# A hybrid layer's first unit: statistics, scaling and rounding of x at separate places, the norm in two parts, first loads in a fixed order

## The chip, the cores and the metric

One Trainium2 chip, one core of it. The metric is the device time of one execution, in microseconds (us). Before the change it is 2423.84 us, the median of three runs (2422.58 to 2424.6).

## What is computed

One decoder layer on x (2048 x 1024, float32): a pre-norm, one combined input projection, a gated DeltaNet branch, a sliding-window attention branch in three groups of four heads, gates and an output projection. The change touches the start: the norm of x and the projections of the attention branch.

```python
h = rms_norm(x, norm_w[layer])
proj = h @ w_in[layer]
...
sq = partial_rope(rms_norm(grp(swa_q), q_norm_w[layer][:, None, :]), cos, sin)
sk = partial_rope(rms_norm(grp(swa_k), k_norm_w[layer][:, None, :]), cos, sin)
sv = grp(swa_v)
```

## The kernel before, in words

TensorE works in a reduced float32 format, so each operand is split into a high part (rounded by ScalarE) and a low part (the rest, by a subtraction on VectorE or GpSimd), and each product is three matmuls: high by high, high by low weight, low by high weight (lines 234 to 236 in `s_proj`).

The attention branch comes first, in 12 **units**, one for each group and head. A unit has 16 **tiles** of 128 tokens. A tile is 24 matmuls of 384 columns (8 k-blocks by 3), issued in four **slots** of two k-blocks each. Behind a tile `s_norm` squares the queries and keys (ScalarE, line 245), copies the values, forms the inverse roots on GpSimd (lines 249 and 251, tile `st`), scales queries and keys out of PSUM on VectorE (line 253, `rec`), rotates 32 columns on GpSimd (lines 261 to 264) and writes the record to DRAM (line 265, `rscr`). `rec` and `st` have two buffers, the PSUM tile `mm` has three. The attention of a finished group reads the records back (`a_load`, lines 273 and 274) and works between the slots of later tiles.

The normalised x does not exist when the kernel starts. The **first unit** makes it, tile by tile, in 16 x events. An event c consists of: the sum of squares of the rows (ScalarE, line 109, `xst`) and its inverse root on GpSimd (lines 110 and 112); a diagonal matrix of these roots (ScalarE, line 116, `dg`); a matmul that spreads them over all partitions (line 120, `tp`); eight scalings of the transposed x (VectorE, line 126, `xc`); the high part (ScalarE, line 131, `hh`, two instructions); the low part (line 135, `hl`: five k-blocks on VectorE, three on GpSimd). Event 0 is written out in `swa`, mixed with the eight blocks of the first unit's weights (`high`, line 186, and `low`, line 189: even blocks on VectorE, odd ones on GpSimd). Events 1 to 15 are called in `swa` between the slots, event c behind the first slot whose number reaches 3.5 (c - 1); `x_event(c)` then issues all at once: the diagonal of event c + 1, the statistics of event c + 2, the load of x for event c + 4, and the matmul, scaling, high and low parts of its own.

The weights of the next unit come through three buffers (`raw`); for unit 2 they are split behind tiles 13 to 15 of the first unit (`w384`, lines 78 and 79).

The order on TensorE, ScalarE, VectorE and GpSimd is the order in which the code issues (`manual_schedule`), and each engine runs its queue in order. The order of the DMAs on SyncE's queue is chosen by the framework's scheduler in the version before.

Of the kernel before, what the change touches and what calls it, by code (L numbers as in the profile page):

```python
# [8 lines left out]
AF = mybir.ActivationFunctionType  # L9
# [6 lines left out]
KT = D // P  # L16
NB = 4
H = 4
# [18 lines left out]
def dr(ap, off, dims):  # L37
    return bass.AP(tensor=ap.tensor, offset=ap.offset + off, ap=[list(d) for d in dims])


class Net:
# [94 lines left out]
                          in1=self.hhf[:, n, k0:k1, c:c + P], op=ALU.subtract)  # L136

    def x_event(self, c):
        if c + 1 < 16:
            self.x_diag(c + 1)  # L140
        if c + 2 < 16:
            self.x_stat(c + 2)
            self.x_nat(c + 4)
        rows = self.x_rows(c)
        self.x_scale(c, rows, 0, KT)
        self.x_high(c, 0, 4)
        self.x_high(c, 4, KT)
# [90 lines left out]
    def s_norm(self, s):  # L238
        nc, sp, g, t = self.nc, self.sp, s["g"], s["t"]
        pr = s["pr"]  # L240
        st = sp.tile([P, 4], F32, name="st", bufs=2)
        rec = sp.tile([P, 3, P], F32, name="rec", bufs=2)
        qk, v = rec[:, 0:2, :], rec[:, 2, :]
        for j in range(2):
            nc.scalar.activation(qk[:, j, :], pr[:, j * P:(j + 1) * P], AF.Square, accum_out=st[:, j:j + 1])  # L245
        nc.scalar.activation(v, pr[:, 256:384], AF.Copy)
        if (s["h"], g) == AB_UNIT:
            nc.vector.tensor_copy(self.ab[:, :, t], pr[:, 384:392])
        nc.gpsimd.tensor_scalar(out=st[:, 0:2], in0=st[:, 0:2], scalar1=1.0 / P, scalar2=EPS,  # L249
                                op0=ALU.mult, op1=ALU.add)  # L250
        nc.gpsimd.tensor_tensor(out=st[:, 2:4], in0=st[:, 0:2], in1=self.mhalf[:, 0:2], op=ALU.pow)  # L251
        for j in range(2):
            nc.vector.scalar_tensor_tensor(out=qk[:, j, :], in0=pr[:, j * P:(j + 1) * P], scalar=st[:, 2 + j:3 + j],  # L253
                                           in1=s["w"][2][:, j, :], op0=ALU.mult, op1=ALU.mult)
# [6 lines left out]
        nc.gpsimd.tensor_tensor(out=t1, in0=x, in1=cb, op=ALU.mult)  # L261
# [3 lines left out]
        nc.sync.dma_start(dr(self.rscr[s["h"]][g], t * P * 384, [[384, P], [1, 384]]), rec.rearrange("p a c -> p (a c)"))  # L265
# [77 lines left out]
    def att_slots(self, step, which):  # L343
        for a in self.att:
            d = step - a["at"]
            if "qk" not in a and (d == 0 or (d == -2 and which == 0)):
                self.a_load(a)
            if which == 0 and d == 2:
                self.a_ptrans(a)
            elif which == 1 and d == 1:  # L350
                self.a_score(a)
            elif which == 2 and d == 2:
                self.a_pv(a)
            elif which == 2 and d == 0:
                self.a_trans(a)
        self.att = [a for a in self.att if step - a["at"] < 4]

    def swa(self, units, wps, xctx):
        nc = self.nc
        step = self.step  # L360
        nu = len(units)
        w0, load, high, low = self.w_first(wps[0](), *units[0])
        w = {0: w0}
        for _ in range(2):
            load()
        self.x_nat(1)
        self.warm(26)
        self.x_stat(0)
        self.x_diag(0)
        rows = self.x_rows(0)  # L370
        load()
        self.x_chan(1)
        load()
        high(0)
        low(0)
        for k in (0, 2):
            self.x_scale(0, rows, k, k + 2)
            self.x_high(0, k, k + 2)
        high(1)
        low(1)  # L380
        self.x_low(0, 0, 4, nc.vector)
        for k in (4, 6):
            self.x_scale(0, rows, k, k + 2)
            self.x_high(0, k, k + 2)
        self.x_low(0, 4, 8, nc.gpsimd)
        self.xc.pop(0)
        self.x_nat(2)
# [16 lines left out]
        nc.sync.dma_start(self.rope, self.i["rope"])  # L404
        nc.sync.dma_start(self.mask, self.i["mask"])
        xq = list(range(1, 16))
        for u in range(nu):
            gen = None
            for t in range(16):
                s = dict(h=units[u][0], g=units[u][1], t=t, pr=None, w=w[u])  # L410
                for j in range(4):
                    self.s_proj(s, (2 * j, 2 * j + 1))
                    if j < 3:
                        self.att_slots(step, j)
                    if u == 0 and xq and 4 * t + j >= 3.5 * (xq[0] - 1):
                        self.x_event(xq.pop(0))
                        if not xq:
                            xctx.close()
# [8 lines left out]
                step += 1  # L427
        self.step = step

    def att_drain(self):  # L430
# [566 lines left out]
    def run(self):  # L997
        from functools import partial
        tc = self.tc
        tile_ = dict(reuse_waits="tile")  # L1000
        pool = lambda st, name, side="left": st.enter_context(tc.tile_pool(name=name, bufs=1, side=side, **tile_))
        self.setup()
        sws, wst, xst, late = ExitStack(), ExitStack(), ExitStack(), ExitStack()
        sp = pool(sws, "sp", "right")
        wpa = pool(wst, "wpa")
        self.x_setup(pool(xst, "xp"))
        self.swa_setup(sp)
# [7 lines left out]
        with tc.manual_schedule(engines={E.PE, E.Activation, E.DVE, E.Pool}):  # L1015
            self.swa([(h, g) for g in (2, 1, 0) for h in range(H)], [lambda: (wpa, 392), lambda: (get_b(), 384)], xst)
# [122 lines left out]
```

## Time and profile before

| | us |
|---|---|
| median of three runs | 2423.84 |
| the profiled execution, its own time | 2421.24 |
| span of its instructions | 2419.4 |
| TensorE busy, whole span | 2354.2 (97%) |
| VectorE, ScalarE, GpSimd busy | 1171.0, 854.3, 847.4 |

The profile is one execution. A line of a timeline is: start, duration, engine (PE is TensorE, DVE VectorE, ACT ScalarE, POOL GpSimd, SPq the DMA queue of SyncE), line of the code, operation, tiles (out<-in), count, and in brackets how long the engine had been idle before it and who released it. In the chain of waits a line is start, duration, what; "issue" is time in which nothing that the profile shows was waited for. A line of a stretch is: from and to, length, then the busy time of each engine with its instruction count in brackets, the granted TensorE clock (1 is full), the DMA engines' mean busy share, and GB/s. A busy engine is not an engine at its peak: the ends of pipelined matmuls are modelled.

### The profile page before, as it was taken

What the parts mean: (1) busy time and instruction counts of PE and PEld (TensorE: products, weight loads), DVE (VectorE), ACT (ScalarE), POOL (GpSimd) and SP (SyncE); (2) the same over time, 40 slices, a digit from 0 to 9 for tenths busy, and PEclk for the clock granted to TensorE, in tenths of its full rate; (3) what the DMA queues carried; (4) which work ended last, traced back from release to release, by engine and by line L of the source; (5) the groups of instructions that cost most, each with busy time, mean ns of one, the idle gap of its engine ahead of it and who ended that gap; (6) DMA issues with size and microseconds to landing.
All of it is one profiled execution on the core that took longest, in us unless ns stands there. A gap on an engine that the chain in (4) does not pass through costs nothing.

```text
span 2419.4 us, 40764 instructions
## 1 busy us (share of the span) xinstructions
PE 2354.2 (97%) x13640; PEld 2138.1 (88%) x13640; DVE 1171.0 (48%) x2835; ACT 854.3 (35%) x3005; POOL 847.4 (35%) x1803
## 2 busy tenths in 40 slices
PE   7799999999999999999999999999999999999999
PEld 6699999999999999988777878888888878889998
DVE  4533343334334333343766665999434442454431
ACT  5433333344444434333665663111133313111110
POOL 5634444434333334310433541111123212432441
PEclk8999999999999999999999999999999999999999
DMA  7443444343334334333544443222566555555542
GB/s 257 135 117 106 118 115 118 98 116 109 98 108 113 100 98 120 92 92 98 128 120 110 114 124 113 75 79 66 185 192 194 179 175 154 165 179 153 153 140 75
DMA packets 378810, 307.31 MB, mean 127 GB/s; under 512 B 61352, under 2 KB 345320, under 8 KB 378216
## 3 DMA queue, kind: packets, MB, share of 16 engines
q1 hardware_dynamic: 378312, 304.64, 43.5%
q8 instruction: 108, 1.77, 0.3%
q14 instruction: 102, 0.84, 0.1%
q10 hardware_dynamic: 288, 0.07, 0.0%
HBM read 187.92 MB, written 116.69 MB: 126 GB/s over the span
## 4 chain that ended last, share of the span: by engine, by line
PE 82%; DMA 6%; DVE 5%; POOL 3%; ACT 2%; issue 2%; SPq 0%; ACTq 0%; DVEq 0%; POOLq 0%
PE mm L234 10%; PE mm L236 10%; PE mm L235 10%; PE mm L489 9%; PE mm L491 8%; PE mm L490 8%; DMA gcb<-gcscr 2%; PE mm L962 2%; PE mm L964 2%; PE mm L963 2%; PE mm L981 2%; PE mm L979 2%; PE mm L980 2%; PE po L323 2%; PE tp L280 2%
## 5 line engine op out<-in xcount | busy, mean ns | idle before, releaser
L234 PE MATMUL mm<-wh,hh 128*128 128x384 f32 (+1 forms) x1536 | 557.2, 363 | 9.7 <-DVE rec L253 5.5
L236 PE MATMUL mm<-wh,hl 128*128 128x384 f32 (+1 forms) x1536 | 521.8, 340 | 7.4 <-DVE hl L135 7.4
L235 PE MATMUL mm<-wl,hh 128*128 128x384 f32 (+1 forms) x1536 | 520.1, 339 | 2.4 <-DVE wl L79 2.4
L489 PE MATMUL mm<-hh,wh 128*128 128x512 f32 x1152 | 464.1, 403 | 0.0
L491 PE MATMUL mm<-hh,wl 128*128 128x512 f32 x1152 | 453.7, 394 | 0.0
L490 PE MATMUL mm<-hl,wh 128*128 128x512 f32 x1152 | 452.3, 393 | 0.0
L253 DVE SCALAR_TENSOR_TENSOR rec<-mm,st,wqk 128x128 f32<-128x128 f32 x384 | 117.2, 347 | 393.5 <-POOL st L251 378.7
L234 PEld LDWEIGHTS mm<-wh,hh 128*128 128x128 f32 x1536 | 291.2, 190 | 16.0 <-issue 4.3
L236 PEld LDWEIGHTS mm<-wh,hl 128*128 128x128 f32 x1536 | 290.6, 189 | 9.7 <-DVE hl L135 9.6
L235 PEld LDWEIGHTS mm<-wl,hh 128*128 128x128 f32 x1536 | 292.3, 190 | 3.2 <-DVE wl L79 2.9
L491 PEld LDWEIGHTS mm<-hh,wl 128*128 128x128 f32 x1152 | 217.0, 188 | 47.1
L489 PEld LDWEIGHTS mm<-hh,wh 128*128 128x128 f32 x1152 | 217.2, 188 | 42.7
L490 PEld LDWEIGHTS mm<-hl,wh 128*128 128x128 f32 x1152 | 217.5, 189 | 41.2
L79 POOL TENSOR_TENSOR wl<-raw,wh 128x512 fp32r<-128x512 f32 (+1 forms) x73 | 104.2, 1438 | 409.0 <-ACT wh L78 409.0
L307 ACT ACTIVATE p<-sc,ol 128x128 f32<-128x128 f32 (+1 forms) x192 | 82.0, 427 | 333.2 <-DVE ol L305 281.6
L249 POOL TENSOR_SCALAR st<-st 128x2 f32<-128x2 f32 x192 | 36.7, 191 | 399.8 <-ACT rec L245 398.4
L245 ACT ACTIVATE rec<-mm 128x128 f32<-128x128 f32 x384 | 102.6, 273 | 177.2 <-PE mm L236 161.3
L962 PE MATMUL mm<-oh,hh 128*128 128x256 f32 x512 | 143.9, 281 | 3.2 <-DVE gt L966 2.9
L963 PE MATMUL mm<-ol,hh 128*128 128x256 f32 x512 | 142.9, 279 | 0.0
L964 PE MATMUL mm<-oh,hl 128*128 128x256 f32 x512 | 142.9, 279 | 0.0
L594 DVE SCALAR_TENSOR_TENSOR acc<-xr,cw,acc 128x512 f32<-128x512 f32 x144 | 121.7, 845 | 41.9 <-ACT acc L592 37.6
L251 POOL TENSOR_TENSOR st<-st,mhalf 128x2 f32<-128x2 f32 x192 | 134.7, 701 | 16.0
(240 smaller groups left out, 4301.3 us busy)
## 6 DMA issues: line engine op xcount, KB each, us to landing
rscr<-rec SPq DMA_DIRECT2D x192, 192.0 KB, 1.9
raw<-in_w_in_dram SPq DMA_DIRECT2D x138, 256.0 KB, 3.1
qk<-rscr SPq DMA_DIRECT2D x192, 128.0 KB, 2.3
gscr<-gt SPq DMA_DIRECT2D x64, 256.0 KB, 2.4
gt<-gscr SPq DMA_DIRECT2D x64, 256.0 KB, 3.4
oscr<-ol SPq DMA_DIRECT2D x192, 65.0 KB, 2.1
oc<-oscr SPq DMA_DIRECT2D x16, 780.0 KB, 5.1
v<-rscr SPq DMA_DIRECT2D x192, 64.0 KB, 2.2
```

Of the source, the lines that this page charges most:

```text
L234: nc.tensor.matmul(pr[:, :w], a, wh[:, k, :w], start=(k == 0), stop=False)
L235: nc.tensor.matmul(pr[:, :w], a, wl[:, k, :w], start=False, stop=False)
L236: nc.tensor.matmul(pr[:, :w], b, wh[:, k, :w], start=False, stop=(k == KT - 1))
L251: nc.gpsimd.tensor_tensor(out=st[:, 2:4], in0=st[:, 0:2], in1=self.mhalf[:, 0:2], op=ALU.pow)
L253: nc.vector.scalar_tensor_tensor(out=qk[:, j, :], in0=pr[:, j * P:(j + 1) * P], scalar=st[:, 2 + j:3 + j], in1=s["w"][2][:, j, :], op0=ALU ...
L489: nc.tensor.matmul(pr, wh[:, k, :], a, start=(k == 0), stop=False)
L490: nc.tensor.matmul(pr, wh[:, k, :], b, start=False, stop=False)
L491: nc.tensor.matmul(pr, wl[:, k, :], a, start=False, stop=(k == KT - 1))
L594: nc.vector.scalar_tensor_tensor(out=acc, in0=xr[:, j:j + 512], scalar=w[:, j:j + 1], in1=acc, op0=ALU.mult, op1=ALU.add)
L962: nc.tensor.matmul(o, self.wbh[:, k, ms], oh[:, k, :], start=(k == b * 4), stop=False)
L963: nc.tensor.matmul(o, self.wbh[:, k, ms], ol[:, k, :], start=False, stop=False)
L964: nc.tensor.matmul(o, self.wbl[:, k, ms], oh[:, k, :], start=False, stop=(k == b * 4 + 3))
```

## The change

- An x event is cut into parts with places of their own. Counted in slots, with q = 3.5 (c - 1): statistics of event c (and the load of x two events on) at q - 5, the diagonal at q - 2, the matmul and the scaling at q, the high and low parts (and the load of the transposed x three events on) at q + 2.
- `s_norm` keeps the squares, the value copy and the inverse roots. The scaling of queries and keys, the rotation and the write become `s_turn`, called behind the second slot of the next tile, ahead of the x parts that are due there. In later units nothing that touches VectorE's or GpSimd's queue lies between the end of a tile and that place, but for the weight splits.
- `a_load`'s early call moves from the first to the second slot, behind `s_turn`.
- The code of event 0 becomes `swa_first`, in which SyncE's order is fixed too. All eight weight blocks are loaded ahead of the x of events 2 and 3; the statistics of event 1 are issued ahead of event 0's second low part and of weight block 3, its diagonal behind block 4 (before: behind block 6); the statistics of event 2 leave this part.
- In one unit, the copy of 8 columns goes from VectorE to ScalarE.

```diff
     def x_event(self, c):
-        if c + 1 < 16:
-            self.x_diag(c + 1)
-        if c + 2 < 16:
-            self.x_stat(c + 2)
-            self.x_nat(c + 4)
-        rows = self.x_rows(c)
-        self.x_scale(c, rows, 0, KT)
+        self.x_scale(c, self.x_rows(c), 0, KT)
+
+    def x_next(self, c):
+        self.x_stat(c)
+        self.x_nat(c + 2)
+
+    def x_parts(self, c):
         self.x_high(c, 0, 4)
         self.x_high(c, 4, KT)
         self.x_low(c, 0, 5, self.nc.vector)
...
         if (s["h"], g) == AB_UNIT:
-            nc.vector.tensor_copy(self.ab[:, :, t], pr[:, 384:392])
+            nc.scalar.activation(self.ab[:, :, t], pr[:, 384:392], AF.Copy)
         nc.gpsimd.tensor_scalar(out=st[:, 0:2], in0=st[:, 0:2], scalar1=1.0 / P, scalar2=EPS,
                                 op0=ALU.mult, op1=ALU.add)
         nc.gpsimd.tensor_tensor(out=st[:, 2:4], in0=st[:, 0:2], in1=self.mhalf[:, 0:2], op=ALU.pow)
+        s["st"], s["rec"] = st, rec
+
+    def s_turn(self, s):
+        nc, sp, g, t = self.nc, self.sp, s["g"], s["t"]
+        pr, st, rec = s["pr"], s["st"], s["rec"]
+        qk = rec[:, 0:2, :]
         for j in range(2):
             nc.vector.scalar_tensor_tensor(out=qk[:, j, :], in0=pr[:, j * P:(j + 1) * P], scalar=st[:, 2 + j:3 + j],
...
-            if "qk" not in a and (d == 0 or (d == -2 and which == 0)):
+            if "qk" not in a and (d == 0 or (d == -2 and which == 1)):
                 self.a_load(a)
...
-        for _ in range(2):
+        for _ in range(3):
             load()
         self.x_nat(1)
+        self.x_chan(1)
+        load()
         self.warm(26)
         self.x_stat(0)
         self.x_diag(0)
         rows = self.x_rows(0)
-        load()
-        self.x_chan(1)
-        load()
         high(0)
         low(0)
...
             self.x_high(0, k, k + 2)
+        high(2)
+        self.x_stat(1)
         self.x_low(0, 4, 8, nc.gpsimd)
         self.xc.pop(0)
-        self.x_nat(2)
-        for k in range(2, 8):
+        low(2)
+        load()
+        for k in range(3, 8):
             if k < 6:
                 load()
             high(k)
             low(k)
-            if k == 3:
-                self.x_stat(1)
-                self.x_chan(2)
-                self.x_nat(3)
-            if k == 6:
+            if k == 4:
                 self.x_diag(1)
-                self.x_stat(2)
-                self.x_nat(4)
-                self.x_chan(3)
+        self.x_nat(2)
+        self.x_chan(2)
+        self.x_nat(3)
...
+        for c in range(1, 16):
+            q = 3.5 * (c - 1)
+            if c > 1:
+                xq += [(max(q - 5, 2.5), self.x_next, c), (max(q - 2, 3), self.x_diag, c)]
+            xq += [(q, self.x_event, c), (q + 2, self.x_parts, c)]
+        xq.sort(key=lambda e: e[0])
+        turn = None
...
                 for j in range(4):
                     self.s_proj(s, (2 * j, 2 * j + 1))
+                    if j == 1 and turn:
+                        self.s_turn(turn)
                     if j < 3:
                         self.att_slots(step, j)
-                    if u == 0 and xq and 4 * t + j >= 3.5 * (xq[0] - 1):
-                        self.x_event(xq.pop(0))
+                    while xq and 4 * t + j >= xq[0][0]:
+                        _, f, c = xq.pop(0)
+                        f(c)
                         if not xq:
                             xctx.close()
                 self.s_norm(s)
+                turn = s
```

More of the change, by code (lines that the diff above doesn't have):

```diff
@@ L356, in att_slots, with swa_first @@
         self.att = [a for a in self.att if step - a["at"] < 4]
-    def swa(self, units, wps, xctx):
+    def swa_first(self, units, wps, xctx):
         nc = self.nc
-        step = self.step
-        nu = len(units)
+        self.swa_setup(self.sp)
+        self.x_setup(self.xp)
         w0, load, high, low = self.w_first(wps[0](), *units[0])
-        w = {0: w0}
-        for _ in range(2):
+        for _ in range(3):
             load()
         self.x_nat(1)
+        self.x_chan(1)
+        load()
         self.warm(26)
@@ L404, in swa, with swa_units @@
         nc.sync.dma_start(self.rope, self.i["rope"])
+        self.x_chan(3)
         nc.sync.dma_start(self.mask, self.i["mask"])
-        xq = list(range(1, 16))
+        return xctx, w0
+    def swa(self, units, wps, xst, pinned):
+        nc = self.nc
+        step = self.step
+        with pinned(True):
+            xctx, w0 = self.swa_first(units, wps, xst)
+        with pinned(False):
+            self.swa_units(units, wps, xctx, w0)
+    def swa_units(self, units, wps, xctx, w0):
+        nc = self.nc
+        step = self.step
+        nu = len(units)
+        w = {0: w0}
+        xq = []
+        for c in range(1, 16):
[5 more added lines that the diff above has]
+        turn = None
         for u in range(nu):
@@ L427, in swa @@
                 step += 1
+        self.s_turn(turn)
         self.step = step
@@ L1003, in run @@
         sws, wst, xst, late = ExitStack(), ExitStack(), ExitStack(), ExitStack()
-        sp = pool(sws, "sp", "right")
+        self.sp = pool(sws, "sp", "right")
         wpa = pool(wst, "wpa")
-        self.x_setup(pool(xst, "xp"))
-        self.swa_setup(sp)
+        self.xp = pool(xst, "xp")
         wpb = []
@@ L1014, in run @@
         E = mybir.EngineType
-        with tc.manual_schedule(engines={E.PE, E.Activation, E.DVE, E.Pool}):
-            self.swa([(h, g) for g in (2, 1, 0) for h in range(H)], [lambda: (wpa, 392), lambda: (get_b(), 384)], xst)
+        pinned = lambda sync: tc.manual_schedule(engines={E.PE, E.Activation, E.DVE, E.Pool} | ({E.SP} if sync else set()))
+        self.swa([(h, g) for g in (2, 1, 0) for h in range(H)], [lambda: (wpa, 392), lambda: (get_b(), 384)], xst, pinned)
         wst.close()
```

## The prediction

> **What bounds the kernel now.** I read the stretches first, because the change acts on the first unit alone: where does TensorE stand still, and when?
>
> ```profile
> 20.60:102.60 82.00, 66.80 (x358) 61.15 (x357) 47.86 (x151) 43.94 (x131) 56.87 (x111) 0.98 0.60 194
> 128.00:1040.00 912.00, 910.20 (x5752) 903.45 (x5751) 355.95 (x1284) 351.90 (x1559) 368.11 (x1050) 1.00 0.38 108
> ```
>
> From 128 us to the end of the attention units TensorE idles for 1.8 of 912 us. There is nothing to win there. From the first event of the loop (20.6) to the last (102.6) it idles for 15.2 us of 82. How fast could a tile go?
>
> ```profile
> 35.37 0.42 PE L234 MATMUL mm<-wh,hh 128*128 128x384 f32 x1
> ...
> 38.42 0.34 PE L236 MATMUL mm<-wh,hl 128*128 128x384 f32 x1
> ```
>
> These are the first and the last of 18 matmuls in a row: 3.05 us over 17 steps, 0.179 us each, so 4.3 us for the 24 of a tile, and 4.45 with an event's own matmul (0.14, an estimate from the gaps around them). That is the floor. What TensorE waits for, in the two longest totals before 240 us:
>
> ```profile
> PE tp L120 <- ACT dg L116: 12.2, 6, 7.3
> PE mm L236 <- DVE hl L135: 7.4, 7, 1.3
> ```
>
> The columns are us in total, times, longest. Both are products of the x events. The chain of waits says how they hang together; this is one turn of it.
>
> ```profile
> 40.19 1.65 POOL hl L135
> 42.20 0.71 POOL st L251
> 42.98 0.23 issue
> 43.21 0.34 DVE rec L253
> 43.55 2.08 DVE xc L126 x8
> 45.65 0.64 ACT hh L131
> 46.35 1.65 POOL hl L135
> ```
>
> A closed loop of 6.16 us, through four engine queues, per tile with an event. GpSimd computes the inverse roots of the queries and keys only behind the event's low part; VectorE's `rec` waits for them; the next event's scaling stands behind `rec`; the high part follows, and then the next low part. Not one engine is full: it is the order that bounds. The loop runs nearly the whole stage:
>
> ```profile
> 20.59 2.16 DVE L126 SCALAR_TENSOR_TENSOR xc<-xc,nw,tp 128x128 f32<-128x128 f32 x8 [0.59 <-PE tp L120]
> ...
> 27.54 2.15 DVE L126 SCALAR_TENSOR_TENSOR xc<-xc,nw,tp 128x128 f32<-128x128 f32 x8
> ...
> 102.50 2.15 DVE L126 SCALAR_TENSOR_TENSOR xc<-xc,nw,tp 128x128 f32<-128x128 f32 x8
> ```
>
> The scalings of events 1 to 15 start from 20.59 to 102.50: 14 steps in 81.9 us. The first takes 6.95, and 11 turns of 6.16 make 67.8. Two steps are left (where 3.5 slots put two events into one tile) with 7.15, so 3.6 each.
>
> **The change part by part: the loop.** Scaling at q and parts at q + 2 let the event's VectorE work and `rec` pass each other, since `rec` now stands behind the second slot of the next tile. `xc` and `hh` leave the loop. What stays is GpSimd's own list, one turn of which was:
>
> ```profile
> 41.93 0.19 POOL L249 TENSOR_SCALAR st<-st 128x2 f32<-128x2 f32 x1
> 42.20 0.70 POOL L251 TENSOR_TENSOR st<-st,mhalf 128x2 f32<-128x2 f32 x1
> 43.63 0.32 POOL L261 TENSOR_TENSOR t<-rec,rope 128x64 f32<-128x64 f32 x1 [0.72 <-DVE rec L253]
> ...
> 44.85 0.19 POOL L110 TENSOR_SCALAR xst<-xst 128x1 f32<-128x1 f32 x1
> 45.12 0.55 POOL L112 TENSOR_TENSOR xst<-xst,mhalf 128x1 f32<-128x1 f32 x1
> ```
>
> The new order on GpSimd is roots, rotation, low part, statistics, next roots. Each with its gap: roots 0.97 (41.93 to 42.90); the wait for `rec`, 0.73, which stays, because in most tiles nothing stands between roots and rotation; rotation 1.22 (43.63 to 44.85); low part 1.74 (40.19 to 41.93); statistics 0.90 (44.85 to 45.67, and a gap). Sum 5.56 us, above TensorE's 4.45, so GpSimd's queue becomes the bound: 0.60 won per turn, 6.6 in 11. TensorE's matmul of the next event is what will then wait, for a diagonal whose root is late in that queue. A second event in one tile costs GpSimd 1.74 + 0.90 = 2.64 and VectorE about 3.0 (2.16 and 0.82, its rows); I leave those two steps at 3.6.
>
> The low part needs a closer look. Its two halves start together: GpSimd's at 46.35 in the chain, VectorE's in the first row here.
>
> ```profile
> 46.31 0.82 DVE L135 TENSOR_TENSOR hl<-xc,hh 128x640 fp32r<-128x640 f32 x1 [0.70 <-ACT hh L131]
> 21.61 1.01 POOL L189 TENSOR_TENSOR wl<-raw,wh 128x384 fp32r<-128x384 f32 x1
> ```
>
> GpSimd's subtraction of 384 columns takes 1.65 beside VectorE's and 1.01 with no such neighbour (second row, while VectorE scales): 0.64 goes on standing aside. In the new order VectorE's half comes right behind `rec`, just where the rotation starts. There the rotation would lose about what the low part wins, at most the 0.82 of VectorE's row against 0.64, which leaves 5.56 to 5.74. If VectorE's half falls on nothing, a turn is 5.56 - 0.64 = 4.92; if it stands in the way of both, 6.2. I take 5.56, because rotation and VectorE's half wait for the same `rec`; the ends are 4.92 and 6.2.
>
> [...]
>
> **The start.**
>
> ```profile
> 12.05 1.26 POOL L135 TENSOR_TENSOR hl<-xc,hh 128x512 fp32r<-128x512 f32 x1 [0.70 <-ACT hh L131]
> ...
> 12.70 1.04 ACT L109 ACTIVATE xt<-xt 128x1024 f32<-128x1024 f32 x1
> 13.27 1.31 POOL L189 TENSOR_TENSOR wl<-raw,wh 128x384 fp32r<-128x384 f32 x1
> ...
> 18.88 0.52 ACT L186 ACTIVATE wh<-raw 128x384 fp32r<-128x384 f32 x1 [3.05 <-DMA raw<-in_w_in_dram]
> ```
>
> And in the chain of waits:
>
> ```profile
> 14.76 4.55 DMA raw<-in_w_in_dram
> ```
>
> Now TensorE waits 7.3 us for event 1's diagonal, which stands on ScalarE behind block 6 (18.88), whose load took 4.55. Behind block 4 it is ready about 15.2. That stall goes; next late is VectorE, where event 1's scaling stands behind block 6's low part. Block 6's load no longer queues behind loads of x: issued 0 to 1 us earlier and with less beside it, it lands 0 to 2.4 earlier; I take 1.4. With rounding and low part, event 1's scaling starts at about 18.3 instead of 20.59.
>
> Against that, event 1's statistics now stand on GpSimd ahead of event 0's low part. The sum of squares ends on ScalarE at 13.9, so the low part moves from 12.05 to 14.8, block 3's from 13.27 to 16.1, and block 7's load, which waits for that buffer, from 14.76 to about 17.3. With 3 to 4.55 for the DMA (3 is an estimate: with no queue beside it), 0.5 and 1.0 for the split, the weights are complete at 21.9 to 23.3; before it was 22.6 (the 21.61 row). Tile 0's end moves by less than 1 us either way at full clock. The x of events 2 and 3 is loaded behind block 7 and lands when ScalarE wants it, about 21.5 to 22.5. Then ScalarE does event 1's high part (1.1), two sums of squares (about 1.15 each with the read of the sum) and the diagonal of event 2, so that event 2's scaling comes at 25.7 to 28.2; I take 26.7 instead of 27.54. **Gain up to event 2: 0.9, range -0.6 to 1.9.** The 2.3 of event 1 are mostly lost again here.
>
> **The end of the unit.** The second unit's weights are split behind tiles 13 to 15.
>
> ```profile
> 114.90 1.41 DVE L79 TENSOR_TENSOR wl<-raw,wh 128x512 fp32r<-128x512 f32 x2
> ```
>
> And on SyncE's queue:
>
> ```profile
> 117.05 0.32 SPq L265 DMA_DIRECT2D rscr<-rec  x1
> 117.47 1.54 SPq L213 DMA_DIRECT2D raw<-in_w_in_dram  x3
> ```
>
> The buffers are free at 115.6 and 116.3, but the loads stand behind tile 14's record write (117.05). With the write half a step later they are ahead of it: 1.2 at most. Against it, the split now stands ahead of `rec` on VectorE, and ScalarE's squares of tile 14 wait for tile 12's record to be written. I take 0.5, range -1 to 2.
>
> **Everything else at nothing.** In units 2 to 12 no other instruction stands between the end of a tile and the second slot, save weight splits, so the queues keep their order; the cover is three PSUM buffers and 4.45 us a tile, and each us that `rec` came later than these would be paid on TensorE. `a_load`, half a step later, is a rival below. The 16 small copies move to an engine that is busy 35% of the time.
>
> **Sum:** 0.9 + 6.6 + 0.5 = 8.0. The profiled execution, 2421.24 (span 2419.4), becomes 2413.2. It lay 2.6 below the median of three runs, 2423.84, so I predict 2415.8 for a median.
>
> **The rivals.**
>
> *Faster: VectorE's low part gets out of GpSimd's way.* For: the halves now need not start together, because VectorE has `rec` ahead of its half. Against: it then meets the rotation. At 4.92 a turn, 11 x 1.24 = 13.6, with the ends 15.0: 2408.8. Chance 0.17.
>
> *No change: the turn stays at 6.2.* Low part and rotation are both hit, or GpSimd waits for `hh`, which is issued two slots later than before. Against: GpSimd lags behind TensorE, so high parts should be ready. Gain 1.4 and less: 2422.4. In this case goes, too, that the scheduler's order on SyncE's queue, free after the start, holds writes or loads back. Chance 0.21.
>
> *Slower: the records arrive too late for the transposes of units 2 to 12.* `a_load` is issued half a step later.
>
> ```profile
> rscr<-rec SPq DMA_DIRECT2D x192, 192.0 KB, 1.9
> ...
> qk<-rscr SPq DMA_DIRECT2D x192, 128.0 KB, 2.3
> ```
>
> From a tile's end: squares, roots, wait and rotation about 3.6, the write 1.9, the read 2.3, and half a step, 2.3, at worst: 10.1. The transposes stand behind the third slot, three steps on, at least 12 us behind the tile's end. It decides from 2 us of further delay on SyncE; each us beyond costs up to 1 us per tile, 176 tiles, and 0.1 us each would already make 2433. Against: the 1.8 us of idle time in 912. Chance 0.07.
>
> **How the numbers follow.** The forecast case has 0.55. The least that I call a difference is 0.2%, 4.85 us, about what a measurement of this kernel can tell. The forecast's own range is 5 to 11 won (the start -0.6 to 1.9, the turn by 0.2 either way), nearly all above 4.85; with the first rival, faster is 0.70. Same is 0.22, slower 0.08. The range takes in the first rival and half of the second: 2407 to 2422.
>
> **What would show it.** Right: scalings of x 5.4 to 5.7 us apart; in the waits, `tp` <- `dg` rises in count; GpSimd's idle time before the rotation stays 0.7; no wait of 7 us before event 1; the stretch from 128 us on as long as before, shifted by 8. Wrong: a turn above 6 or below 5.1; TensorE waiting for `qk` at line 280; event 2's scaling later than 28 us; or squares that wait for a record's write in many tiles.

## The result, and the profile after

The changed kernel takes 2407.57 us (median of four runs, 2406.04 to 2409.19); the kernel before, run beside it, 2423.21 (four runs). The ratio is 0.9935, with a 95% interval of 0.9918 to 0.9952: 15.6 us won, where 8 were forecast. The profiled execution after took 2406.66, span 2404.7.

Where the time went is read from four landmarks that both kernels have. The steps between them are the three terms of the prediction's sum.

| landmark, us from the start | before | after |
|---|---|---|
| scaling of event 2 starts | 27.54 | 27.07 |
| scaling of event 15 starts | 102.50 | 93.08 |
| last weight split for unit 2 starts | 122.18 | 109.54 |
| first transposes of the attention (`tp` <- `qk`) | 133.74 | 119.61 |

The first stage won 0.5, the loop from event 2 to event 15 took 66.0 instead of 75.0 and won 8.95, and the end of the unit won 4.7: 14.1 in sum. Behind it TensorE stands as little as it did, as the stretches of after show (the second is the prediction's stretch from 128 us, shifted by 14):

```profile
15.60:93.20 77.60, 66.80 (x339) 61.31 (x338) 48.35 (x152) 44.66 (x132) 58.17 (x114) 0.93 0.71 239
...
114.00:1026.00 912.00, 910.41 (x5763) 903.74 (x5762) 356.85 (x1271) 354.32 (x1576) 348.81 (x1052) 1.00 0.38 108
```

From the first event to the last TensorE now idles for 10.8 us of 77.6, and for 1.6 of 912 later. The waits of TensorE before 240 us, in total, times, longest:

```profile
PE tp L120 <- ACT dg L116: 11.8, 11, 3.6
PE mm L236 <- DVE hl L135: 1.5, 2, 0.9
```

The wait for the low part fell from 7.4 us to 1.5, and the one for `rec` is gone. The diagonal is waited for eleven times instead of six, by 11.8 us in all: it is what is late next. The timeline of after shows one of the three plain turns of the loop (one event to one rotation, as in the prediction's list), GpSimd first and then VectorE:

```profile
67.60 1.01 POOL L135 TENSOR_TENSOR hl<-xc,hh 128x384 fp32r<-128x384 f32 x1
68.70 0.19 POOL L110 TENSOR_SCALAR xst<-xst 128x1 f32<-128x1 f32 x1
...
69.61 0.19 POOL L249 TENSOR_SCALAR st<-st 128x2 f32<-128x2 f32 x1
...
71.31 0.83 POOL L267 TENSOR_TENSOR t<-rec,rope 128x64 f32<-128x64 f32 x1 [0.72 <-DVE rec L259]
...
72.93 1.02 POOL L135 TENSOR_TENSOR hl<-xc,hh 128x384 fp32r<-128x384 f32 x1
...
70.62 0.61 DVE L259 SCALAR_TENSOR_TENSOR rec<-mm,st,wqk 128x128 f32<-128x128 f32 x2 [1.91 <-POOL st L251]
71.15 0.81 DVE L135 TENSOR_TENSOR hl<-xc,hh 128x640 fp32r<-128x640 f32 x1
71.88 2.15 DVE L126 SCALAR_TENSOR_TENSOR xc<-xc,nw,tp 128x128 f32<-128x128 f32 x8
```

GpSimd's list from one low part to the next is 5.33 us: low part 1.10 (67.60 to 68.70), statistics 0.91, roots 0.98 (69.61 to 70.59), the wait for `rec` 0.72, rotation 1.62 (71.31 to 72.93). In this turn VectorE waits for the roots (1.91), GpSimd waits for `rec` (0.72), and nobody waits for `hh`. The scalings:

```profile
27.07 2.16 DVE L126 SCALAR_TENSOR_TENSOR xc<-xc,nw,tp 128x128 f32<-128x128 f32 x8 [5.12 <-PE tp L120]
...
66.56 2.15 DVE L126 SCALAR_TENSOR_TENSOR xc<-xc,nw,tp 128x128 f32<-128x128 f32 x8
...
93.08 0.60 DVE L126 SCALAR_TENSOR_TENSOR xc<-xc,nw,tp 128x128 f32<-128x128 f32 x2
```

The 13 steps from 27.07 to 93.08 hold two short ones (3.59 and 4.22); the other eleven are 5.29 on average. Only three of them are plain turns of 5.32 or 5.33 (from 66.56 on); the others lie between 4.42 and 7.09. What differs there is shown by GpSimd's low part of event 6:

```profile
50.44 1.66 POOL L135 TENSOR_TENSOR hl<-xc,hh 128x384 fp32r<-128x384 f32 x1
```

It starts 0.04 behind VectorE's half and takes 1.66, as before the change, and so it is in seven of the 14 events from 2 to 15. In five of these GpSimd had stood for `hh` first, for 0.4 to 1.6 us. Where the low part comes between the roots and the rotation, the wait for `rec` falls away: four of the twelve rotations in the loop do not wait. Now the end of the unit, first as it was before, in rows not shown yet:

```profile
111.95 0.28 ACT L245 ACTIVATE rec<-mm 128x128 f32<-128x128 f32 x1 [4.23 <-DMA rscr<-rec]
...
122.18 0.69 DVE L79 TENSOR_TENSOR wl<-raw,wh 128x512 fp32r<-128x512 f32 x1 [0.23 <-ACT wh L78]
...
123.41 0.52 PE L236 MATMUL mm<-wh,hl 128*128 128x384 f32 x1
123.73 0.52 PE L234 MATMUL mm<-wh,hh 128*128 128x384 f32 x1
```

And in the changed kernel:

```profile
102.98 0.28 ACT L245 ACTIVATE rec<-mm 128x128 f32<-128x128 f32 x1 [4.56 <-DMA rscr<-rec]
...
104.32 1.90 DVE L79 TENSOR_TENSOR wl<-raw,wh 128x512 fp32r<-128x512 f32 x3 [1.66 <-ACT wh L78]
...
105.04 1.57 SPq L213 DMA_DIRECT2D raw<-in_w_in_dram  x3
...
109.54 0.69 DVE L79 TENSOR_TENSOR wl<-raw,wh 128x512 fp32r<-128x512 f32 x1 [0.16 <-ACT wh L78]
109.56 0.44 PE L234 MATMUL mm<-wh,hh 128*128 128x384 f32 x1 [1.71 <-ACT wh L78]
110.57 0.34 PE L236 MATMUL mm<-wh,hl 128*128 128x384 f32 x1
110.74 0.34 PE L234 MATMUL mm<-wh,hh 128*128 128x384 f32 x1
```

In both kernels ScalarE's squares of tile 14 are held up by an older record's write, for 4.2 and 4.6 us. Before, all the rest hangs on these squares: roots, `rec`, then the splits (114.90, 2.95 behind the squares), then the freed buffers' loads (117.47, 5.52 behind), then the last split (10.23 behind). After, the splits do not stand behind `rec`: they start 1.34 behind the squares, the loads 2.06, the last split 6.56. That is 3.67 us. The squares themselves come 0.45 later behind event 15 than before (9.90 instead of 9.45). And before, TensorE ran about ten matmuls at half pace after its wait of 2.27 us for the last weights (123.41 to 123.73 is a pitch of 0.32; in the changed kernel, after 1.71, it is 0.17, 110.57 to 110.74). From the last split to the transposes it is 1.49 less (11.56 and 10.07), about what ten matmuls lose at that pitch. 3.67 - 0.45 + 1.49 = 4.71.

### The profile page after: what moved, and what is told of

Read it like the earlier page. It is cut to its first block, busy times and chain, and to the rows that moved or that the text cites. A ratio compares the mean times of both kernels' runs of the same rounds, so it can differ in the third digit from the quotient of the medians.

```text
span 2404.7 us, 40630 instructions
## 1 busy us (share of the span) xinstructions
PE 2356.5 (98%) x13640; PEld 2140.6 (89%) x13640; DVE 1171.0 (49%) x2819; ACT 855.6 (36%) x3021; POOL 827.0 (34%) x1803
## 4 chain that ended last, share of the span: by engine, by line
PE 85%; DMA 5%; POOL 3%; DVE 3%; ACT 2%; issue 2%; SPq 0%; ACTq 0%; POOLq 0%; DVEq 0%
PE mm L236 10%; PE mm L234 10%; PE mm L235 10%; PE mm L520 9%; PE mm L522 9%; PE mm L521 9%; PE mm L1012 2%; PE mm L1010 2%; PE mm L1011 2%; DMA gcb<-gcscr 2%; PE mm L993 2%; PE mm L995 2%; PE mm L994 2%; PE po L329 2%; PE tp L286 2%
```

## The experiments

The theory: the turn is won only by both parts together, x in pieces and the norm in two, because each alone leaves a loop through all four queues; and the end is won by the splits no longer standing behind `rec`. The rivals: one part alone is the gain (in particular: the first loads), or GpSimd's queue is not what sets the new turn. All runs by the same landmarks, in us; "loop" is event 2 to event 15, "end" is event 15 to the first transposes. The time is a median where a ratio is given with it below, otherwise one run, which says little (the kernel before had medians of 2421.1 to 2424.0 beside these runs).

| kernel | event 2 | loop | end | transposes | time |
|---|---|---|---|---|---|
| before | 27.5 | 75.0 | 31.2 | 133.7 | 2423.2 |
| changed | 27.1 | 66.0 | 26.5 | 119.6 | 2407.6 |
| norm whole | 29.2 | 72.2 | 31.9 | 133.3 | 2419.6 |
| x in one | 30.8 | 71.8 | 26.6 | 129.3 | 2415.9 |
| first part old | 27.2 | 65.9 | 28.2 | 121.3 | 2404.2 |
| norm ahead of the splits | 28.1 | 66.3 | 31.2 | 125.6 | 2408.7 |
| low part on VectorE | 27.8 | 62.0 | 27.5 | 117.3 | 2404.6 |
| low part on GpSimd | 27.7 | 74.7 | 27.4 | 129.9 | 2412.2 |
| event 3's statistics later | 25.0 | 67.6 | 26.5 | 119.1 | 2405.5 |
| event 3's statistics later, low part on VectorE | 24.3 | 64.2 | 27.5 | 116.0 | 2404.6 |
| statistics in the gap | 24.9 | 65.1 | 28.0 | 118.0 | 2406.7 |
| statistics in the gap, low part on VectorE | 24.4 | 64.4 | 25.9 | 114.7 | 2402.3 |
| the same, event 4's statistics back | 24.5 | 61.4 | 27.4 | 113.3 | 2397.0 |

**The norm whole, everything else changed.** `s_turn` follows `s_norm` at once.

```diff
                     self.s_proj(s, (2 * j, 2 * j + 1))
-                    if j == 1 and turn:
-                        self.s_turn(turn)
...
                 self.s_norm(s)
-                turn = s
+                self.s_turn(s)
```

> The changed kernel with one part undone: the scaling of queries and keys, the rotation and the record's write stand right behind the inverse roots again; x at its separate places and the fixed first loads stay. Theory A (the half step is what breaks the loop of 6.16 us, and it is what lets the weight splits of unit 2 pass in front of rec): most of the gain goes, the second unit's first tile ends at 121 to 127 us instead of 112.3 (before: 126.4), the span is 2413 to 2420. Rival B (the separate places of x break the loop by themselves): 112 to 115 us, span 2405 to 2408.

2419.56 (10 runs) against 2423.99 (15 runs): ratio 0.9984, 0.9975 to 0.9994. A turn in its timeline, first GpSimd, then VectorE:

```profile
72.55 1.64 POOL L135 TENSOR_TENSOR hl<-xc,hh 128x384 fp32r<-128x384 f32 x1 [1.59 <-ACT hh L131]
...
69.13 0.61 DVE L259 SCALAR_TENSOR_TENSOR rec<-mm,st,wqk 128x128 f32<-128x128 f32 x2 [2.87 <-POOL st L251]
69.66 2.15 DVE L126 SCALAR_TENSOR_TENSOR xc<-xc,nw,tp 128x128 f32<-128x128 f32 x8
72.50 0.83 DVE L135 TENSOR_TENSOR hl<-xc,hh 128x640 fp32r<-128x640 f32 x1 [0.70 <-ACT hh L131]
```

The old loop is closed again: `rec`, then the scaling, then the high part, then both halves of the low part at the same moment (72.50 and 72.55, 1.64 instead of 1.02), then statistics and roots. GpSimd stands 1.59 for `hh`; a turn in this stretch is 7.05 (69.66 to 76.71); the 13 steps go from 3.6 to 8.7. And the end is 31.9, as before: of the 14.1 us, 0.4 are left at the transposes, as theory A had it (the profiled span, 2421.3, is 1.3 above its range). The median is 4.4 below before, more than the landmarks say. The profiled execution is the slowest of the ten (2423.23), and 2.85 us are won between the transposes and the first DeltaNet matmul, in a stretch that is taken up under "Nothing elsewhere" below.

**x in one place, everything else changed.** Diagonal of c + 1, statistics of c + 2, scaling, high and low part at q; the statistics of event 2 are issued at the end of the first part.

```diff
-            if c > 1:
-                xq += [(max(q - 5, 2.5), self.x_next, c), (max(q - 2, 3), self.x_diag, c)]
-            xq += [(q, self.x_event, c), (q + 2, self.x_parts, c)]
+            xq.append((q, self.x_whole, c))
```

> The changed kernel with another part undone: an x event issues everything at one place again, as before the change; the norm in two parts and the fixed first loads stay. Theory A: the loop is broken without the places, but GpSimd's low part and the statistics fall worse; the second unit's first tile ends at 114 to 119 us, span 2407 to 2412. Rival B: nearly the old loop, 121 to 126 us, span 2414 to 2419.

2415.85 (6 runs), ratio 0.9972, 0.9959 to 0.9984. Its waits of TensorE (`rec` is line 267 here):

```profile
PE mm L242 <- ACT hh L131: 6.9, 2, 5.4
PE mm L244 <- DVE hl L135: 6.5, 7, 1.3
PE mm L242 <- DVE rec L267: 5.5, 4, 1.7
```

The waits of before are back, for `hl` and for `rec` (the PSUM tile that it frees), and most turns are 6.14 to 6.18 again. The 5.4 for `hh` is one wait, at 27.3 in the first tiles. The loop wins 3.1 and event 2 loses 3.3. But the end is 26.6: the whole of its gain of 4.5 at the transposes is the end term. This is nearly the old loop, as rival B had it, and not theory A. At the transposes, in one execution of each, the two halves of the change are worth 0.4 and 4.5 alone and 14.1 together: 9.2 need both. By the medians it is 4.4 and 8.1 alone and 15.6 together, so that only 3.1 need both. That the loop needs both is seen in its turns; how much of the whole time that is worth stays open.

**The first part as before**, with the changed order behind it (the first loads, event 1's statistics and diagonal where they were, SyncE's order free there).

```diff
-            if k == 4:
+            if k == 3:
+                self.x_stat(1)
+                self.x_chan(2)
+                self.x_nat(3)
+            if k == 6:
                 self.x_diag(1)
...
-        with pinned(True):
+        with pinned(False):
             xctx, w0 = self.swa_first(units, wps, xst)
```

> The changed kernel with the third part undone: the code of event 0 and the first loads in the order of before, SyncE's queue free. Event 2's scaling started at 27.07 us after the change and at 27.54 before it. Theory A (the first part is worth at most 1 us): span within 2 us of 2404.7, event 2's scaling at 26.5 to 28. Rival C (the early start carries a good part, by a clock that rises sooner and by x that is there in time): span 2408 to 2412.

TensorE stands 7.3 us for event 1's diagonal again, and event 1's scaling is at 20.81. Yet event 2's is at 27.18 and event 15's at 93.08, the very time of the changed kernel. The first loads are worth nothing here, as theory A had it (the profiled span, 2402.4, is 0.3 below its range). The transposes are 1.6 later: after a wait of 1.88 us for the last weights, nine matmuls ran at half pace (0.32 from one to the next; below, under the hardware), about 1.3 us of it.

**The norm ahead of the splits.** For the tiles behind which weights are split, `s_turn` follows at once.

```diff
                 self.s_norm(s)
                 turn = s
+                if u == 0 and t >= 13:
+                    self.s_turn(s)
+                    turn = None
                 self.att_add(s, step)
```

> The changed kernel, but behind tiles 13, 14 and 15 of the first unit the second part of the norm comes at once, ahead of unit 2's weight splits. Theory A (4.7 us of the gain come at the end of the first unit, because splits no longer stand behind rec on VectorE nor their loads behind the record's write, and the wait is then too short to halve the clock): the scaling of event 15 stays at 93, the second unit's first tile ends at 115 to 117.5 us instead of 112.3, span 2407.5 to 2410. Rival D (the end is earlier only because the events end earlier): no more than 0.5 us later, span 2404 to 2405.5.

```profile
106.28 0.61 DVE L259 SCALAR_TENSOR_TENSOR rec<-mm,st,wqk 128x128 f32<-128x128 f32 x2 [2.11 <-POOL st L251]
106.80 1.41 DVE L79 TENSOR_TENSOR wl<-raw,wh 128x512 fp32r<-128x512 f32 x2
108.95 0.32 SPq L271 DMA_DIRECT2D rscr<-rec  x1
...
109.37 1.54 SPq L213 DMA_DIRECT2D raw<-in_w_in_dram  x3
```

The order of before in the changed kernel: the splits behind `rec`, the loads behind the record's write. The loop keeps its 66.3, the end is 31.2 as before, 4.7 more than in the changed kernel. So the end term is this order, with the half pace (0.32) that followed its longer wait (3.56 us for the last weights, against 1.71 and a pitch of 0.17), and it is separate from the loop. The second unit's first tile ends at about 118.2, above theory A's 115 to 117.5, and the span, 2406.9, is 0.6 below its range; rival D is out.

**The low part on one engine.** In the changed kernel, all eight k-blocks on VectorE, or all on GpSimd.

```diff
-        self.x_low(c, 0, 5, self.nc.vector)
-        self.x_low(c, 5, KT, self.nc.gpsimd)
+        self.x_low(c, 0, KT, self.nc.vector)
```

> The changed kernel with GpSimd's share of the x events' low part (three of eight k-blocks) given to VectorE; everything else as in the changed kernel. Theory A (after the change GpSimd's queue sets the turn: roots, wait, rotation, low part, statistics, 5.33 us): without the low part (1.02 and a gap) a turn falls to about 4.2 on GpSimd, TensorE's 4.45 or VectorE's sum (2.15 + 0.53 + about 1.3) becomes the bound, and the scaling of event 15 starts at 83 to 90 us instead of 93.1. Rival E (the waits for diagonals come from the order on ScalarE, GpSimd only stands in it): 92 to 96 us.

```profile
74.39 1.23 POOL L266 TENSOR_TENSOR t<-rec,rope 128x64 f32<-128x64 f32 x1 [0.72 <-DVE rec L258]
...
74.23 1.21 DVE L135 TENSOR_TENSOR hl<-xc,hh 128x1024 fp32r<-128x1024 f32 x1
```

The plain turn is 4.75 (scalings at 70.62, 75.37, 80.11), 0.58 less: GpSimd is rid of 1.10 of low part, and its rotation, whose first instruction now stands beside a subtraction of 1.21 and takes 1.23 instead of 0.83, is 2.15 from start to next instead of 1.62. Theory A had counted on 4.2 there, and on TensorE or VectorE as the new bound; GpSimd stays it. The loop is 62.0.

> The opposite: GpSimd does the whole low part of the x events, VectorE none. 384 columns took it 1.02 us with nothing in the way, so 1024 take about 2.65; the rotation no longer meets VectorE's half (0.83 to 0.32). Theory A: a turn grows by 2.65 - 1.02 - 0.51 = 1.1 us, and event 15's scaling starts 9 to 15 us later, at 102 to 108. Rival E: 92 to 97 us.

```profile
71.94 0.33 POOL L266 TENSOR_TENSOR t<-rec,rope 128x64 f32<-128x64 f32 x1 [0.72 <-DVE rec L258]
...
73.05 2.38 POOL L135 TENSOR_TENSOR hl<-xc,hh 128x1024 fp32r<-128x1024 f32 x1
...
71.78 2.15 DVE L126 SCALAR_TENSOR_TENSOR xc<-xc,nw,tp 128x128 f32<-128x128 f32 x8
```

The plain turn is 6.18, 0.85 more: low part 2.46 with its gap instead of 1.10, and the rotation 1.11 instead of 1.62. Here VectorE scales while GpSimd rotates, and the rotation's first instruction takes 0.33. So what holds it up in these kernels is VectorE's subtraction (0.83 and 1.23 beside one), not its scaling. In both runs the plain turn is the sum of GpSimd's rows, with 0.72 of waiting in it: its queue sets the pace there. Event 15 starts at 89.78 and 102.47, each inside theory A's range and outside rival E's.

**The start, event 3's statistics behind event 2's diagonal.** ScalarE stood 2.27 us for event 3's x (row at 25.05 in the changed kernel, under the start below), with event 2's diagonal queued behind it.

```diff
-                xq += [(max(q - 5, 2.5), self.x_next, c), (max(q - 2, 3), self.x_diag, c)]
+                xq += [(max(q - 5, 2.5 if c == 2 else 3.2), self.x_next, c), (max(q - 2, 3), self.x_diag, c)]
```

> The changed kernel with the statistics of event 3 issued behind the diagonal of event 2 instead of ahead of it. In the changed kernel ScalarE stands 2.27 us for event 3's x while the diagonal of event 2 is queued behind it, and TensorE waits 3.58 for that diagonal. Theory A (the start's gain at event 1 is lost in this wait): event 2's scaling starts at 24 to 25.5 us instead of 27.07; how much of it lasts to event 15 is GpSimd's affair: 0 to 2 us earlier than 93.1. Rival F (it is the record of event 2's own x and its root that is late): 26.5 to 27.5.

Event 2 comes at 24.95, 2.1 earlier; event 15 at 92.58, 0.5 earlier. Most of it is gone by event 5 (40.71 for 41.12): VectorE's waits for GpSimd's roots ahead of `rec` grow, between 27 and 60 us, from 4.6 to 7.5. With the first loads the time was lost sooner: event 1 is at 15.67 in the changed kernel and at 20.81 with the old first part, event 2 at 27.07 and 27.18. In neither case did time won at the start reach event 15.

> Both of these edits: the whole low part on VectorE, and event 3's statistics behind event 2's diagonal. Theory A: event 2's scaling at 24 to 25.5, event 15's at 81 to 88 us; the span 2394 to 2401. Rival E and F: as in the changed kernel, span 2402 to 2408.

With the low part on VectorE as well, event 15 is at 88.49 and the transposes at 115.99, 3.6 earlier than in the changed kernel. The span is 2402.8, only 1.9 less, and event 15 is 0.5 later than theory A allowed. The span lies above its range and in the rivals'; one run does not tell 1.9 from the spread.

**The statistics in the gap.** GpSimd's 0.72 between roots and rotation is idle, and the statistics are 0.91. They are moved to the first slot of a tile, so that they stand between the two.

```diff
-                xq += [(max(q - 5, 2.5), self.x_next, c), (max(q - 2, 3), self.x_diag, c)]
+                xq += [(2.5 if c == 2 else max((q - 5) // 4 * 4, 3.2), self.x_next, c), (max(q - 2, 3), self.x_diag, c)]
```

> The changed kernel with the statistics of an x event always behind the first slot of a tile (event 3's behind the diagonal of event 2), so that on GpSimd they stand between the roots of a tile and its rotation. Theory A (in a full turn GpSimd idles 0.72 us until rec is there, and that idle time is in the chain): the 0.91 of the statistics fills it, a turn falls from 5.33 to about 4.6, event 2's scaling starts at 24 to 25.5 and event 15's at 86 to 90 us instead of 93.1. Rival G (the idle time is slack, something else is late): turns stay at 5.2 to 5.4, event 15's at 92 to 94.

```profile
71.02 0.19 POOL L110 TENSOR_SCALAR xst<-xst 128x1 f32<-128x1 f32 x1
71.29 0.54 POOL L112 TENSOR_TENSOR xst<-xst,mhalf 128x1 f32<-128x1 f32 x1
71.79 0.70 POOL L267 TENSOR_TENSOR t<-rec,rope 128x64 f32<-128x64 f32 x1
```

No idle time is left ahead of the rotation, and the plain turn is 4.43 (67.80, 72.23, 76.66, 81.08): TensorE's own 4.45, and TensorE does not stand at all from 66 to 82. But event 3's scaling falls to 34.24, and the loop as a whole wins only 0.9. The next version has the low part on VectorE too.

> The same, and the whole low part on VectorE. Theory A: GpSimd's list is then about 4.0 to 4.3 us with the rotation held up by VectorE, VectorE's own 3.9, TensorE's 4.45 a tile: event 15's scaling starts at 82 to 88 us, the first transposes of the attention at 109 to 115 instead of 119.6; 3 to 10 us below the changed kernel in the median. Rival G: as with the low part on VectorE alone and event 3's statistics later, 88 to 89 and 116.

2402.34 (2397.71 to 2406.11, 6 runs), ratio 0.9920, 0.9905 to 0.9935; the plain turn is 4.07. Event 15 is at 88.82, where rival G had it; the transposes and the median are in theory A's range. Event 3 is as late as in the run before, and ScalarE's rows tell why:

```profile
30.89 1.06 ACT L109 ACTIVATE xt<-xt 128x1024 f32<-128x1024 f32 x1 [5.36 <-DMA xt<-in_x_dram]
31.95 0.39 ACT L116 ACTIVATE dg<-ident,xst 128x128 f32<-128x128 f32 x1
```

It stood 5.36 us for the x of event 4, and the diagonal behind it is event 3's, whose root was long there.

> The changed kernel itself once more, for a comparison on the same chip and in the same hour: 2404 to 2410 us in the median; in the profile the first transposes of the attention at 119.6 within 1.5 us, since the events' turns are set by queues of fixed order and only the DMAs vary.

The changed kernel beside it: 2405.92 (2402.54 to 2410.01, 6 runs), ratio 0.9937, 0.9921 to 0.9953. The first result stands. From the kernel with both edits it differs by 3.6, and the two ranges overlap.

**Event 4's statistics back**, in the kernel with both edits.

```diff
-                xq += [(2.5 if c == 2 else max((q - 5) // 4 * 4, 3.2), self.x_next, c), (max(q - 2, 3), self.x_diag, c)]
+                xq += [({2: 2.5, 3: 3.2, 4: 5.5}.get(c, (q - 5) // 4 * 4), self.x_next, c), (max(q - 2, 3), self.x_diag, c)]
```

> The changed kernel with the whole low part on VectorE and the statistics at the first slot of a tile, except event 4's, which stand where the changed kernel has them. Theory: with the statistics at the first slot of every tile, ScalarE stood 5.36 us for event 4's x with event 3's diagonal queued behind it, so that event 3's scaling came at 34.55 and event 4's at 40.86. With event 4's statistics back, event 3's scaling starts at 29 to 31 us, event 4's at 35 to 37, event 15's at 83 to 86 instead of 88.8, the first transposes of the attention's unit at 109 to 112 instead of 114.7, and the median is 2395 to 2400. Rival: the events behind catch up anyway, because the queues of GpSimd and VectorE and not the late diagonal set the pace of the first four turns: event 15 at 87.5 to 89, the transposes at 114 to 115.5, the median at 2401 to 2404.

2397.01 (2395.1 to 2399.33, 5 runs), ratio 0.9894, 0.9876 to 0.9911, clear of the changed kernel's interval: the best version, 25 us below before. Its interval overlaps that of the kernel with both edits (0.9905 to 0.9935), so what event 4's edit adds is read from the landmarks. Its scalings, and one low part on VectorE:

```profile
30.42 2.15 DVE L126 SCALAR_TENSOR_TENSOR xc<-xc,nw,tp 128x128 f32<-128x128 f32 x8
36.92 2.15 DVE L126 SCALAR_TENSOR_TENSOR xc<-xc,nw,tp 128x128 f32<-128x128 f32 x8
...
72.79 2.14 DVE L126 SCALAR_TENSOR_TENSOR xc<-xc,nw,tp 128x128 f32<-128x128 f32 x8
76.85 2.14 DVE L126 SCALAR_TENSOR_TENSOR xc<-xc,nw,tp 128x128 f32<-128x128 f32 x8
81.36 2.15 DVE L126 SCALAR_TENSOR_TENSOR xc<-xc,nw,tp 128x128 f32<-128x128 f32 x8
84.20 1.23 DVE L135 TENSOR_TENSOR hl<-xc,hh 128x1024 fp32r<-128x1024 f32 x1 [0.70 <-ACT hh L131]
85.87 2.15 DVE L126 SCALAR_TENSOR_TENSOR xc<-xc,nw,tp 128x128 f32<-128x128 f32 x8
```

Events 3, 4 and 15 came where the theory put them. The turn is 4.07 at first and then 4.51, and in both it is VectorE's: at 4.07 scaling, `rec` and low part follow each other with 0.18 of waiting; at 4.51 the low part stands ahead of `rec` and waits 0.70 for the high part of the scaling just done. TensorE's matmul for event 14 starts at 77.78, 3.6 ahead of the scaling. GpSimd's list is the bound no more. Only the transposes, at 113.30, miss their 109 to 112: the wait for the last weights (1.88) was followed by nine matmuls at half pace (0.32), about 1.3 us.

## Why the prediction was right, and where it was not

**The direction and the mechanism** were right: faster, by the loop of the first unit, with GpSimd's list as the new bound and the diagonal as TensorE's next wait. The time lies inside the range, by 0.6 us at its lower end. 2415.8 was too high because two terms of the sum were too small. That it is off by no more is not to the sum's credit alone: in the profiled executions about 3 us of the difference are half pace of TensorE (about 1.5 at the end of the unit, about 1.5 at 964.84), which the sum did not hold. The gain of 15.6 is nearly the 15.0 of the first rival, but not by the first rival's sum, eleven turns of 4.92.

**The loop: 6.6 forecast, 8.95 measured.** The step that failed is "the rotation would lose about what the low part wins", and with it one price for every turn. In the plain turns the low part won 0.64 (1.10 with its gap for 1.74), as the second of the two rows had it. The rotation lost only 0.40, since VectorE's half starts 0.16 ahead of it and holds up one of four instructions (0.83 for 0.32). So the plain turn is 5.33, between the forecast and the first rival. Eleven turns of 5.29 instead of 6.16 are 9.6; two short steps, left at 3.6 each, took 7.81, which gives 0.65 back.

The regular turn of the forecast did not come, though. By its own signs (scalings 5.4 to 5.7 apart; wrong above 6 or below 5.1) none of the 13 steps is right: none lies between 5.4 and 5.7 (the plain ones are 5.32 or 5.33), one is 7.09, above 6, and five besides the two short ones lie below 5.1. The steps that it left at 3.6, where two events fall into one tile, took 4.92 and 5.32; the short ones now are others (events 8 to 9 and 9 to 10). And the wait for `rec`, "which stays", is gone in four of twelve rotations, while seven low parts keep their 1.65. That the average of the long steps comes to 5.29, beside a plain turn of 5.33, is a coincidence of turns of several kinds; what held is that GpSimd's queue sets the pace: with the low part taken off it, or all put on it, the loop went from 66.0 to 62.0 and 74.7.

The first instruction of the rotation took 0.83 and 1.23 beside subtractions of 0.81 and 1.21, and 0.33 beside the scalings; why a subtraction holds it up and a scaling does not, the runs do not show. The price can be read more closely: against 0.32 the held-up instruction lost 0.51 and 0.91 where 0.65 and 1.05 of the subtraction were left, 0.14 less each time. The prediction's pair (0.64 lost, 0.78 left) and the one with the statistics in the gap (0.38 lost, 0.52 left) give the same 0.14.

**The end: 0.5 forecast, 4.7 measured.** The failed step is "1.2 at most". It looked at SyncE's queue alone, where the loads stood 1.2 behind free buffers, and not at what set the time at which the buffers came free: splits behind `rec`, `rec` behind roots, roots behind squares that a record's write held up. Taking `rec` out from between moved the splits by 1.6, the loads by 3.5 and the last split by 3.7; the run with the norm ahead of the splits gave all of it back. The prediction's counter-argument, squares that wait for a record, is real (4.56), but it was there before (4.23). Of the 4.7, about 1.5 is half pace after the wait, which the profiled execution of before had and that of after had not.

**The start: 0.9 forecast, 0.47 measured**, with event 2 at 27.07 for 26.7. The stall of 7.3 us went, as said, and the next thing late is not what I named. TensorE now stands here, in the changed kernel:

```profile
25.05 1.06 ACT L109 ACTIVATE xt<-xt 128x1024 f32<-128x1024 f32 x1 [2.27 <-DMA xt<-in_x_dram]
...
26.54 0.49 PE L120 MATMUL tp<-dg,ones 128*128 128x128 f32 x2 [3.58 <-ACT dg L116]
```

I had both sums of squares ahead of this diagonal, but took the x of event 3 to be there when wanted; it came 2.3 later. The two runs on this stage show that it hardly mattered.

**Nothing elsewhere** held for the records: no wait for `qk`, and the squares wait for a record only twice. The rival of late records did not come. But from the transposes to the first DeltaNet matmul before took 910.4 us and after 908.7; the other twelve profiled versions took 907.6 to 908.4. Of these 1.8 us, 0.2 is a shorter wait (for `pT`, 1.80 at 964.84 before, 1.58 at 950.50 after, 0.5 to 1.1 in five others). The rest is half pace behind that wait: before, ten matmuls ran at a pitch of 0.32, with a granted clock of 0.79 over the next 8 us, and after none did (0.17, clock 1.00). It is one execution of before, so this part of the gain need not come each time. From there to the end the profiled executions took 1372 to 1380, with no order in it: the gain goes from 15.9 to 14.7 there, and I put no cause to it.

## What to carry to other kernels

Where a loop runs through several engines' queues and no engine is full, follow it until it closes: cutting it at one place moved 0.4 or 4.5 us here at the landmarks, and cutting it at both moved 14.1 (4.4, 8.1 and 15.6 in the medians). A queue is priced by everything that stands in it, so ask of each long-waiting instruction what is ready behind it: a split behind a `rec`, a diagonal behind a sum of squares whose x had not landed (a wait of 2.27 us in the changed kernel, of 5.36 with the statistics in the gap and the low part on VectorE). And when an operation is moved off the one that it collided with, look up what it lands on: here the collision cost the rotation 0.51 us beside a subtraction of 0.81, 0.91 beside one of 1.21, and 0.38 where the rotation started 0.29 behind one of 0.81 instead of 0.16.

## What the runs showed of the hardware

After TensorE's wait of 1.65 to 1.88 us for the last weights of unit 2 some matmuls ran at half pace in five runs, and in six none did. In each of these kernels TensorE then has the rest of the tile's matmuls ready. After waits of 1.70 (two runs), 1.71, 1.73, 1.79 and 1.84 us the pitch stayed 0.17. After 1.65, 1.78, 1.82, 1.88 and 1.88 it was 0.32 for some eight to ten matmuls (with 1.78, the low part on VectorE, only after some seven at full pace), as it was for eight to thirteen after the four waits of 2.09 to 3.72 at the end of the unit (before, the norm whole, the norm ahead of the splits). In the timeline of the kernel with event 4's statistics back:

```profile
101.84 0.44 PE L233 MATMUL mm<-wh,hh 128*128 128x384 f32 x1 [1.88 <-ACT wh L78]
...
103.05 0.52 PE L235 MATMUL mm<-wh,hl 128*128 128x384 f32 x1
103.37 0.52 PE L233 MATMUL mm<-wh,hh 128*128 128x384 f32 x1
```

The granted clock from 108 to 122 us was 0.88 where it happened (before, and with the first part old) and 1.00 where it did not (after). Once the half pace followed two shorter waits close together: in the changed kernel's loop TensorE idled 0.87 and 1.25 us between 61.6 and 64.7, and from 65.0 to 68.1 the granted clock was 0.50. One such fall cost an estimated 1.3 to 1.5 us (nine or ten matmuls at 0.32 instead of 0.175), and most ends of 27.4 to 28.2 in the table are the ones with it, those of 25.9 to 26.6 the ones without; the low part on GpSimd has 27.4 without it, and what made up the rest was not shown. The length of the wait alone does not sort these runs: 1.65 us was followed by half pace, 1.84 was not. What else decides, they do not show.
